# Four key chunks of an attention projection computed as seven block products in the queries' list

## The chip, the cores and the metric

The kernel runs on one core of one Trainium2 chip. A core has a matrix engine (PE, TensorE), a vector engine (DVE, VectorE), an activation engine (ACT, ScalarE), a general one (POOL, GpSimd), a queue engine that starts transfers (SP) and 16 DMA engines. Matmuls write to PSUM, eight banks of 128 partitions by 512 floats; everything else works from SBUF. The metric is the device time of one execution in microseconds, the median of several runs; less is better.

## The reference

One inference step of a decoder trunk with two layers, in float32, on 512 prompt tokens and 8 x 4 new tokens of sequences that have 256 tokens behind them. All 544 tokens go through the weights together.

```python
# layer 0: Conformer convolution; layer 1: stick-breaking attention; each followed by a gated ConvFFN
h = rms_norm(x, norm_mix[i])
x = x + mixer(h)
h = rms_norm(x, norm_ffn[i])
x = x + (silu(causal_dwconv(h @ w_gate)) * (h @ w_up)) @ w_down

# the attention's projection: D = 1024, 16 heads of 64
qkv = (h @ attn_w_qkv[a]).reshape(b, t, 3, N_HEADS, HEAD_DIM)
z = einsum('bqhd,bkhd->bhqk', q, k) * HEAD_DIM ** -0.5 + bias      # strictly causal
log_fail = where(valid, log_sigmoid(-z), 0)
after = cumsum(log_fail, axis=3, reverse=True) - log_fail
out = einsum('bhqk,bkhd->bqhd', exp(log_sigmoid(z) + after), v)
```

The rows of K and V of all new tokens are outputs. The 8 sequences attend to their past through a paged cache: 16 pages of K and 16 of V, each 128 tokens by 1024 numbers.

## The kernel before

**Operands.** Tokens stand in the free dimension: `xT`, `XH` and `XL` are 128 partitions x 8 chunks x 544 tokens. A float32 product is made from three matmuls of a faster type: weights are split into `whi` (a rounded copy by ScalarE, line 397) and `wlo` (the rest, by VectorE, line 400), the input into `XH` and `XL`, and `whi XH + whi XL + wlo XH` is summed in PSUM. A chunk of 128 outputs with 1024 inputs takes 8 x 3 matmuls for each of two token stretches, `SA` (256 columns) and `SB` (288).

**Weights.** `raws` is the list of loads, 1 MB each for a pair of chunks, through two SBUF buffers (`RAW_BUFS`); a load is started on SP (line 360) as soon as the last split of the load two places ahead has read its buffer. `specs` is the list of splits, through five buffers (`SPLIT_BUFS`). `both` enters two plain splits for a pair, `quad` four for a pair in the seven-product form.

**Seven products.** `products` (in `ffn`) computes a pair of chunks from a 2 x 2 division: input chunks 0 to 3 and 4 to 7, the two output chunks of the pair, and tokens 0 to 271 and 272 to 543. Sums of weight blocks (`sums`, VectorE) and of token blocks (`inputs`, giving `TH` and `TL`) go through seven products of 12 matmuls with 272 columns; three PSUM tiles hold them, and `put` combines them: a ScalarE copy, or a VectorE addition onto what is there. A plain pair takes 96 matmuls, this one 84. The ConvFFN's chunks and query chunks 4 to 7 (`query_quad`) are made so; query chunks 0 to 3 are plain (`PLAINQ`).

**Order.** The work of a stage is collected as operations in a `Plan`, which orders them before the program is written by estimated costs, readiness and the length of the chain behind each; the order of each engine is then fixed. The first ConvFFN and `queries` (its last product, the norm, the queries) are one list. A second list, the attention list, follows with a plan of its own that starts as if all engines were free. It holds: the projections of keys and values as matmuls that fill gaps (`project`, `plan.fill`, lines 2125 to 2127; order in `TURNS`); `keys` (copy to `kT`, then `to_rows`: turned by PE into the one PSUM bank `one`, copied by VectorE to one of two tiles `kr`, line 2169, and stored); `page_logits` (each of 16 K pages gathered by POOL into one of three tiles, line 2017, turned in two halves into the one bank `t`, line 2245, copied by VectorE or ScalarE, line 2252, and multiplied, line 2263); `decode_weights`; the prompt's attention by pairs of heads (`pair`: logits `z`, line 2387, exponentials, scans on VectorE, line 2417, weights turned in `t`, line 2429, products with V, line 2449); and `sequence`, the V pages. The second ConvFFN follows.

The splits that the attention list needs first are prepared by the end of the queries' list, since each finished weight slot prepares the one five places on (`used`).

Of the kernel before, what the change touches and what calls it, by code (L numbers as in the profile page):

```python
# [19 lines left out]
NC = D // P  # L20
SEQ = 512
# [21 lines left out]
MORE = 3  # L43
CONV_RAWS = 12
PLAINQ = 4

PASSES = ((0, 4), (4, 6), (10, 6), (16, 6))
FFN_CHUNKS = 6
# [4 lines left out]
U_POST = 1.0  # L53
# [196 lines left out]
def tile_trunk(  # L250
# [9 lines left out]
    dve, act, pool, pe = nc.vector, nc.scalar, nc.gpsimd, nc.tensor  # L260
# [35 lines left out]
    def quad(w, c):  # L296

        raws.append(cols2(w, 0, NC, c))
        specs.extend((len(raws) - 1, k, k == 4, NC) for k in (0, 2, 3, 4))
# [29 lines left out]
    for c in range(0, NC, 2):  # L329
        if c < PLAINQ:  # L330
            both(attn_w_qkv[0], 0, NC, c)
        else:
            quad(attn_w_qkv[0], c)
    TURNS = [("k", 0), ("k", 1), ("v", 0)] + [x for c in range(NC) for x in (("k", c + 2), ("v", c + 1)) if x[1] < NC]
    kv = {}
    for f, c in TURNS:
        if (f, c // 2) not in kv:
# [380 lines left out]
    plan = Plan(E_CONV, 0.12, CONV_SHIFTS)  # L718
# [384 lines left out]
    for c in range(0, NC, 2):  # L1103
        pt = psum("av")
# [196 lines left out]
    def ffn(l, before, after):  # L1301
# [455 lines left out]
        def queries(s):  # L1757
# [115 lines left out]
            for c2 in range(PLAINQ, NC, 2):  # L1873
                query_quad(c2, range(s, s + 4))
                s += 4
            xs = [("x", c, h) for c in range(NC) for h in range(2)]
            plan.op("sp", 5.0, lambda: nc.sync.dma_start(out=xsave, in_=xflat), r=[*xs, "normed1"], w=["saved"])
            plan.op("dve", 0.6, decode_columns, w=["tables"])
# [221 lines left out]
    def dcost(n):  # L2100
        return 0.09 + n * 1.1e-3

    def acost(n):
        return 0.1 + n * 0.95e-3
# [54 lines left out]

    def keys(c, h):  # L2160
        c0, n = (SA, SB)[h]
        pt = project(k0 + TURNS.index(("k", c)), h)
        plan.op("act", acost(256), lambda: act.copy(kT[:, c, c0:c0 + 256], pt()[:, :256]),  # L2163
                r=[pt], w=[("k", c, h)] + ([("ktp", i) for i in range(4)] if c >= 4 else []))
        if h:
            plan.op("act", 0.2, lambda: act.copy(kT_s[:, c, :], pt()[:, 256:n]), r=[pt], w=[("kT_s", c)])
        rows, src = to_rows(lambda b: kT[:, c, c0 + b * P:c0 + (b + 1) * P], [("k", c, h)])
        kr = sbuf("kr", 2 * P, 2)
        plan.op("dve", 0.38, lambda: dve.tensor_copy(kr().rearrange("p (b d) -> p b d", b=2), src()), r=[rows], w=[kr])
        plan.op("sp", 3.0, lambda: nc.sync.dma_start(out=kpv[:, 2 * h:2 * h + 2, c * P:(c + 1) * P],  # L2170
                                                     in_=kr().rearrange("p (b d) -> p b d", b=2)), r=[kr])
# [408 lines left out]
```

## Time and profile before

Three runs took 1270.61 to 1270.97 us, median 1270.66. The profile is of one execution; it gives its span, from the first to the last instruction, and no time beside it.

| | us |
|---|---|
| median of the runs | 1270.66 |
| span of the profiled execution | 1268.1 |
| PE, DVE, ACT busy in it | 1257.2, 1004.7, 717.5 |
| 600.0 to 633.5: last part of the queries' list | 33.5 |
| 633.5 to 723: attention list until the decode weights are turned | 89.5 |
| 723 to 845: rest of the attention list | 122 |

A row of the profile names engine, line of the kernel, operation, output and inputs. A matmul's duration (0.28 us) is longer than the step to the next (0.12 us), since matmuls are pipelined: a PE that shows as busy may still be waiting a little between two of them. What counts is the distance between starts. A wait is put down to the engine that released it.

### The profile page before, as it was taken

To read this page: it belongs to the slowest core of one execution; us is meant where nothing else is said; L and a number is where in the kernel's file an instruction comes from. 1 tells how busy PE (TensorE), PEld (TensorE's weight loads), DVE (VectorE), ACT (ScalarE), POOL (GpSimd) and SP (SyncE) were. 2 spreads that over 40 slices of the span, in tenths; PEclk is the share of its full clock that TensorE was granted. 3 is DMA by queue.
4 is the path that set the end of the run, shared out by engine and by line. 5 is a ranking of instruction groups with operands and counts; after the bars stand their busy time and mean duration, and the time that the engine had idled before them with its cause. 6 is when DMAs were issued, how large, how long until landed. Compare 5 with 4: busy or idle time off the path is not lost.

```text
span 1268.1 us, 26470 instructions
## 1 busy us (share of the span) xinstructions
PE 1257.2 (99%) x10846; PEld 1207.7 (95%) x10846; DVE 1004.7 (79%) x1696; ACT 717.5 (57%) x1436; POOL 166.0 (13%) x291
## 2 busy tenths in 40 slices
PE   9999999999999999999999999999999999999998
PEld 8997699999999999999989888999999999999998
DVE  7999876979987887869865589766988987886863
ACT  7794584635655455445564598754646645455453
POOL 5000014101001000002042143200111001000000
PEclk9999999999999999999999999999999999999999
DMA  7455423133233233244354443342123233232221
GB/s 221 131 165 156 119 69 115 35 100 102 92 112 99 74 112 115 62 144 172 116 185 154 152 144 132 119 145 73 62 85 117 91 96 117 67 119 91 85 77 72
DMA packets 119179, 142.39 MB, mean 112 GB/s; under 512 B 5101, under 2 KB 110245, under 8 KB 118786
## 3 DMA queue, kind: packets, MB, share of 16 engines
q1 hardware_dynamic: 110350, 111.89, 28.2%
q0 software_dynamic: 8704, 28.80, 7.0%
q8 instruction: 85, 1.39, 0.5%
q14 instruction: 36, 0.29, 0.1%
q10 hardware_dynamic: 4, 0.01, 0.0%
HBM read 129.34 MB, written 12.18 MB: 112 GB/s over the span
## 4 chain that ended last, share of the span: by engine, by line
PE 88%; DVE 9%; ACT 1%; issue 1%; DMA 0%; DVEq 0%; ACTq 0%
PE acc L1627 5%; PE acc L1626 5%; PE acc L1625 5%; PE acc L755 4%; PE acc L756 4%; PE acc L757 4%; PE av L892 3%; PE tr L1627 3%; PE tr L1626 3%; PE tr L1625 3%; PE av L1401 3%; PE av L1402 3%; PE av L1403 3%; PE tr L1401 3%; PE tr L1402 3%; PE tr L1403 3%
## 5 line engine op out<-in xcount | busy, mean ns | idle before, releaser
L397 ACT CAST whi<-raw 128x1024 fp32r<-128x1024 f32 (+2 forms) x247 | 224.3, 912 | 122.2 <-PE av L1402 25.1
L400 DVE TENSOR_TENSOR wlo<-raw,whi 128x1024 fp32r<-128x1024 f32 (+2 forms) x247 | 259.1, 1052 | 26.6 <-ACT whi L397 24.9
L755 PE MATMUL acc<-XH,whi 128*128 128x288 f32 (+1 forms) x384 | 112.7, 294 | 0.0
L757 PE MATMUL acc<-XH,wlo 128*128 128x288 f32 (+1 forms) x384 | 110.3, 287 | 0.9 <-DVE wlo L400 0.9
L756 PE MATMUL acc<-XL,whi 128*128 128x288 f32 (+1 forms) x384 | 110.3, 287 | 0.0
L1401 PE MATMUL av<-HH,whi 128*128 128x288 f32 (+1 forms) x280 | 83.3, 298 | 0.4 <-DVE xT L1716 0.4
L1627 PE MATMUL acc<-TH,wlo 128*128 128x272 f32 x288 | 83.0, 288 | 0.0
L1626 PE MATMUL acc<-TL,whi 128*128 128x272 f32 x288 | 82.7, 287 | 0.0
L1625 PE MATMUL acc<-TH,whi 128*128 128x272 f32 x288 | 82.7, 287 | 0.0
L1402 PE MATMUL av<-HL,whi 128*128 128x288 f32 (+1 forms) x280 | 82.6, 295 | 0.0
L2125 PE MATMUL acc<-XH,whi 128*128 128x256 f32 (+1 forms) x264 | 82.0, 311 | 0.6 <-ACT kT L2163 0.6
L1403 PE MATMUL av<-HH,wlo 128*128 128x288 f32 (+1 forms) x280 | 82.3, 294 | 0.0
L1661 ACT COPY G<-acc 128x272 f32<-128x272 f32 (+1 forms) x72 | 26.8, 372 | 94.7 <-PE acc L1627 94.7
L1401 PE MATMUL tr<-HH,whi 128*128 128x256 f32 (+1 forms) x280 | 79.1, 283 | 0.0
L1402 PE MATMUL tr<-HL,whi 128*128 128x256 f32 (+1 forms) x280 | 78.9, 282 | 0.0
L1403 PE MATMUL tr<-HH,wlo 128*128 128x256 f32 (+1 forms) x280 | 78.5, 280 | 0.0
L2127 PE MATMUL acc<-XH,wlo 128*128 128x256 f32 (+1 forms) x264 | 75.8, 287 | 0.0
L2126 PE MATMUL acc<-XL,whi 128*128 128x256 f32 (+1 forms) x264 | 75.8, 287 | 0.0
L755 PEld LDWEIGHTS acc<-XH,whi 128*128 128x128 f32 x384 | 72.2, 188 | 1.4 <-issue 0.4
L757 PEld LDWEIGHTS acc<-XH,wlo 128*128 128x128 f32 x384 | 72.1, 188 | 1.1 <-DVE wlo L400 1.1
L756 PEld LDWEIGHTS acc<-XL,whi 128*128 128x128 f32 x384 | 72.2, 188 | 0.3
L1564 DVE SCALAR_TENSOR_TENSOR cv<-G,fprm,cv 128x560 f32<-128x560 f32 x88 | 69.5, 797 | 0.5
(465 smaller groups left out, 4372.7 us busy)
## 6 DMA issues: line engine op xcount, KB each, us to landing
raw<-in_ffn_w_gate_dram SPq DMA_DIRECT2D x22, 1024.0 KB
raw<-in_ffn_w_up_dram SPq DMA_DIRECT2D x22, 1024.0 KB
raw<-in_ffn_w_down_dram SPq DMA_DIRECT2D x24, 768.0 KB
raw<-in_attn_w_qkv_dram SPq DMA_DIRECT2D x12, 1024.0 KB
raw<-in_conv_w_in_dram POOLq DMA_DIRECT2D x6, 1024.0 KB, 8.7
rep<-glu SPq DMA_DIRECT2D x36, 142.0 KB
raw<-in_conv_w_out_dram POOLq DMA_DIRECT2D x4, 1024.0 KB, 7.0
raw<-in_ffn_w_down_dram SPq DMA_DIRECT2D x8, 512.0 KB
```

What stands on the lines that cost most here:

```text
L397: act.copy(hi[:, k, :], src[:, k])
L400: dve.tensor_tensor(lo[:, k, :], src[:, k], hi[:, k, :], op=ALU.subtract)
L755: pe.matmul(o, hi[:, k, :], XH[:, k, c0:c0 + n], start=(k == 0), stop=False)
L756: pe.matmul(o, hi[:, k, :], XL[:, k, c0:c0 + n], start=False, stop=False)
L757: pe.matmul(o, lo[:, k, :], XH[:, k, c0:c0 + n], start=False, stop=(k == NC - 1))
L1401: pe.matmul(o, hi[:, j + k, :], xh, start=(start and k == 0), stop=False, **kw)
L1402: pe.matmul(o, hi[:, j + k, :], xl, start=False, stop=False, **kw)
L1403: pe.matmul(o, lo[:, j + k, :], xh, start=False, stop=(stop and k == len(xs) - 1), **kw)
L1625: pe.matmul(o, hi[:, j + k, :], xh, start=(start and k == 0), stop=False, **kw)
L1626: pe.matmul(o, hi[:, j + k, :], xl, start=False, stop=False, **kw)
L1627: pe.matmul(o, lo[:, j + k, :], xh, start=False, stop=(k == 3), **kw)
L2125: pe.matmul(o, hi[:, k, :], XH[:, k, c0:c0 + n], start=(k == 0), stop=False)
```

## The change

Key chunks 0 to 3 leave the attention list's projections and are made at the end of the queries' list as two pairs of seven block products, right behind the query pairs. They use the token-half sums `TH` and `TL` that the query pairs use. `key_quad` copies and combines the products into `kT`, and copies the new tokens' columns to `kT_s`. The turning of the key rows for the output and their store stay in the attention list; for these chunks they now have nothing to wait for there.

```diff
+EARLY_K = 4
...
+    for c in range(0, EARLY_K, 2):
+        quad(attn_w_qkv[0], NC + c)
-    TURNS = [("k", 0), ("k", 1), ("v", 0)] + [x for c in range(NC) for x in (("k", c + 2), ("v", c + 1)) if x[1] < NC]
+    TURNS = [("v", 0)] + [x for c in range(NC) for x in (("k", c + 2), ("v", c + 1))
+                          if x[1] < NC and (x[0] == "v" or x[1] >= EARLY_K)]
...
+            def key_quad(c2, slots):
+                def put(what, p):
+                    what = what.split()
+                    i, h = (int(x) - 1 for x in what[-1])
+                    c, (c0, n) = c2 + i, HALVES[h]
+                    dst = lambda: att["kT"][:, c, c0:c0 + n]
+                    w = [("kT", c, h)]
+                    if what[0] == "keep" or what[0] == "12":
+                        plan.op("act", acost(n), lambda: act.copy(dst(), p()[:, :n]), r=[p], w=w, urgent=U_POST)
+                    else:
+                        plan.op("dve", dcost(n), lambda: dve.tensor_tensor(
+                            dst(), p()[:, :n], dst(), op=SIGN[what[0]]), r=[p], w=w, urgent=U_POST)
+
+                products(slots, (("acc",) * 3, ("tr", "av", "tr"))[c2 // 2 % 2], put)
+                for c in (c2, c2 + 1):
+                    plan.op("act", 0.2, lambda c=c: act.copy(att["kT_s"][:, c, :], att["kT"][:, c, SEQ:]), r=[("kT", c, 1)])
+
+            for c2 in range(0, EARLY_K, 2):
+                key_quad(c2, range(s, s + 4))
+                s += 4
...
     def keys(c, h):
         c0, n = (SA, SB)[h]
-        pt = project(k0 + TURNS.index(("k", c)), h)
-        plan.op("act", acost(256), lambda: act.copy(kT[:, c, c0:c0 + 256], pt()[:, :256]),
-                r=[pt], w=[("k", c, h)] + ([("ktp", i) for i in range(4)] if c >= 4 else []))
-        if h:
-            plan.op("act", 0.2, lambda: act.copy(kT_s[:, c, :], pt()[:, 256:n]), r=[pt], w=[("kT_s", c)])
+        if c >= EARLY_K:
+            pt = project(k0 + TURNS.index(("k", c)), h)
+            plan.op("act", acost(256), lambda: act.copy(kT[:, c, c0:c0 + 256], pt()[:, :256]),
+                    r=[pt], w=[("k", c, h)] + ([("ktp", i) for i in range(4)] if c >= 4 else []))
+            if h:
+                plan.op("act", 0.2, lambda: act.copy(kT_s[:, c, :], pt()[:, 256:n]), r=[pt], w=[("kT_s", c)])
```

Up to the first query products the order of every engine is as before, and from the end of the attention list on too. Three places in between. In the rows, lines of the new kernel from `keys` on are 25 or 26 higher; numbers behind names tell buffers apart.

PE, from the end of the queries' list to the first pages (`acc`: a projection; `one`: rows of K turned; `z`: logits; `t`, `dz`: halves of a page). Before:

```order
L1627 MATMUL av_7965<-THq,wlo_7923 128x272
L2125 MATMUL acc_8072<-XH,whi_7941 128x256
...
L2127 MATMUL acc_8097<-XH,wlo_7942 128x288
L2245 MATMUL t_8105<-ident,xT 128x128 x4
L2245 MATMUL dz_8110<-ident,xT 128x128 x4
L2155 MATMUL one_8116<-ident,kT 128x128 x2
L2125 MATMUL acc_8097<-XH,whi_7941 128x288
...
L2127 MATMUL acc_8097<-XH,wlo_7942 128x288
L2245 MATMUL t_8130<-ident,xT 128x128 x4
```

And now:

```order
L1631 MATMUL tr_8197<-THq,wlo_8140 128x272
L2180 MATMUL one_8306<-ident,kT 128x128 x2
L2413 MATMUL z_8309<-kT,qT 128x512
L2413 MATMUL z_8311<-kT,qT 128x512
L2180 MATMUL one_8316<-ident,kT 128x128 x2
L2271 MATMUL t_8322<-ident,xT 128x128 x4
L2271 MATMUL dz_8327<-ident,xT 128x128 x4
L2180 MATMUL one_8333<-ident,kT 128x128 x2
L2271 MATMUL t_8340<-ident,xT 128x128 x4
L2180 MATMUL one_8346<-ident,kT 128x128 x2
L2271 MATMUL t_8352<-ident,xT 128x128 x4
L2150 MATMUL acc_8358<-XH,whi_8159 128x256
```

Thirty projection matmuls stood ahead of the first page half, and six behind the first row turn; now the first projection comes after ten rows of turns and logits.

VectorE, at the same place (`wlo`: a weight split; `kr`: the copy of turned key rows). Before:

```order
L400 TENSOR_TENSOR wlo_7993<-raw_7926,whi_7992 128x1024
L1867 SCALAR_TENSOR_TENSOR qT<-av_7965,qT 128x272
L400 TENSOR_TENSOR wlo_8023<-raw_7963,whi_8022 128x1024
L400 TENSOR_TENSOR wlo_8027<-raw_7926,whi_8026 128x1024
L2252 COPY kT<-t_8105 128x4x128
L2169 COPY kr_8127<-one_8116 128x256
```

And now:

```order
L404 TENSOR_TENSOR wlo_8192<-raw_8042,whi_8191 128x1024
L1891 TENSOR_TENSOR kT<-tr_8197,kT 128x272
L404 TENSOR_TENSOR wlo_8225<-raw_8144,whi_8224 128x1024
L1891 TENSOR_TENSOR kT<-tr_8197,kT 128x272
L404 TENSOR_TENSOR wlo_8257<-raw_8195,whi_8256 128x1024
L404 TENSOR_TENSOR wlo_8261<-raw_8144,whi_8260 128x1024
L2195 COPY kr_8313<-one_8306 128x256
L2195 COPY kr_8319<-one_8316 128x256
L2278 COPY kT<-t_8322 128x4x128
L2195 COPY kr_8338<-one_8333 128x256
L2278 COPY kT<-t_8340 128x4x128
```

In both orders the last splits of the queries' list stand ahead of the first copies of the attention list; the copies are now two of key rows ahead of the first page half.

PE, at the end of the stretch with the K pages (`t` from `e`: a block of the prompt's weights turned; the `dz` row: the page logits). Before:

```order
L2245 MATMUL t_8964<-ident,xT 128x128 x4
L2125 MATMUL acc_8940<-XH,whi_8500 128x256
...
L2127 MATMUL acc_8940<-XH,wlo_8501 128x256
L2429 MATMUL t_8983<-ident,e_8439 128x128 x4
L2125 MATMUL acc_8988<-XH,whi_8500 128x288
...
L2127 MATMUL acc_8988<-XH,wlo_8501 128x288
L2429 MATMUL t_9002<-ident,e_8439 128x128 x4
L2263 MATMUL dz_8802<-kT,xT 32x256 x8
```

And now:

```order
L2271 MATMUL t_8984<-ident,xT 128x128 x4
L2150 MATMUL acc_8959<-XH,whi_8256 128x288
...
L2152 MATMUL acc_8959<-XH,wlo_8257 128x288
L2271 MATMUL t_8998<-ident,xT 128x128 x4
L2271 MATMUL t_9010<-ident,xT 128x128 x4
L2455 MATMUL t_9017<-ident,e_8560 128x128 x4
L2289 MATMUL dz_8878<-kT,xT 32x256 x8
```

Twelve projection matmuls stood between the turns; now the last two halves and a block of weights follow each other.

## The prediction

> **What bounds the kernel now.** I read the head of the page first, then the chain, then the stages around the change.
>
> ```profile
> span 1268.1 us, 26470 instructions
> PE 1257.2 (99%) x10846; PEld 1207.7 (95%) x10846; DVE 1004.7 (79%) x1696; ACT 717.5 (57%) x1436; POOL 166.0 (13%) x291
> PE 88%; DVE 9%; ACT 1%; issue 1%; DMA 0%; DVEq 0%; ACTq 0%
> 620.00:633.50 13.50, 13.01 (x104) 12.79 (x103) 9.28 (x12) 7.80 (x13) 0.66 (x3) 1.00 0.47 157
> 633.50:640.00 6.50, 6.50 (x57) 6.50 (x56) 4.22 (x6) 3.56 (x5) 4.54 (x6) 1.00 0.33 109
> 640.00:680.00 40.00, 40.00 (x349) 34.41 (x348) 27.75 (x38) 26.82 (x46) 12.38 (x15) 1.00 0.51 164
> 680.00:723.00 43.00, 42.45 (x396) 38.76 (x394) 18.26 (x29) 17.36 (x35) 8.81 (x10) 1.00 0.55 169
> 723.00:845.00 122.00, 121.48 (x1314) 107.64 (x1313) 98.81 (x148) 95.64 (x172) 34.02 (x39) 1.00 0.43 140
> PE acc L2125 <- ACT kT L2163: 0.6, 1, 0.6
> ```
>
> The stage rows give, after the colon, length, PE, PEld, DVE, ACT and POOL busy, clock, DMA share, GB/s. PE is the bound: 88% of the chain, and full in every stage. The queries' list ends at 633.5; the attention list follows. From 633.5 to 723, where the 16 key pages are turned, the list of waits has a single one on PE, 0.6 us (last row). So each matmul less is worth its issue time, but only while PE keeps something to issue: VectorE and ScalarE are under 70% busy there because projection matmuls lie between the dependent steps. That filling is what the change takes away.
>
> **What a matmul costs.** PE rows of the timeline, start and duration:
>
> ```profile
> 625.23 0.28 PE L1625 MATMUL av<-THq,whi 128*128 128x272 f32 x1
> ...
> 629.60 0.29 PE L1627 MATMUL av<-THq,wlo 128*128 128x272 f32 x1
> ...
> 630.38 0.40 PE L1625 MATMUL av<-XH,whi 128*128 128x272 f32 x1 [0.49 <-ACT qT L1865]
> ...
> 633.50 0.28 PE L2125 MATMUL acc<-XH,whi 128*128 128x256 f32 x1
> ...
> 637.13 0.60 PE L2245 MATMUL t<-ident,xT 128*128 128x128 f32 x4
> 637.56 0.60 PE L2245 MATMUL dz<-ident,xT 128*128 128x128 f32 x4
> 638.00 0.38 PE L2155 MATMUL one<-ident,kT 128*128 128x128 f32 x2
> ...
> 644.79 1.13 PE L2387 MATMUL z<-kT,qT 64*128 64x512 f32 x4
> 645.85 0.66 PE L2245 MATMUL t<-ident,xT 128*128 128x128 f32 x4
> ```
>
> From 625.23 to 629.60 lie 35 steps: 0.125 us for 272 columns, the mean of the 256 and 288 that a chunk's two stretches have. A chunk pair took 2 x 48 = 96 matmuls, 12.0 us, and takes 7 x 12 = 84, 10.5 us. Two pairs save 24 matmuls: **-3.0 us**. The order of PE's program has exactly 24 rows fewer, so the change does what it says. What the products add elsewhere is priced by these rows (min/median/max, ns):
>
> ```profile
> L1364 DVE TENSOR_TENSOR Sq<-raw x2: 1217/1218/1218, 601.8 to 617.5; 128x1024 f32<-128x1024 f32 x2
> L1367 DVE TENSOR_TENSOR raw<-Sq,raw x2: 684/685/686, 606.8 to 619.3; 128x512 f32<-128x512 f32 x2
> L400 DVE TENSOR_TENSOR wlo<-raw,whi 128x1024 fp32r<-128x1024 f32 x6 | 7.3, 1222 | 0.5 <-ACT whi L397 0.5
> L397 ACT CAST whi<-raw 128x1024 fp32r<-128x1024 f32 x7 | 7.4, 1051 | 3.3 <-DVE raw L1369 1.2 <-PE av L1402 0.8 <-ACT whi L397 0.5
> L1867 DVE SCALAR_TENSOR_TENSOR qT<-acc,qT x3: 432/434/434, 615.4 to 624.4; 128x272 f32<-128x272 f32 x3
> L1865 ACT ACTIVATE qT<-acc x4: 384/395/401, 610.8 to 622.4; 128x272 f32<-128x272 f32 x4
> ```
>
> A pair asks VectorE for sums 1.22 + 2 x 0.69, splits 3 x 1.22 + 0.69 and three combinations of 0.43: 8.2 us, and ScalarE for casts 3 x 1.05 + 0.6, four copies of 0.39 and two small ones: 5.7. Both fit into the 10.5 us of PE: hidden, and if the cover failed, only the excess would cost. The 0.49 us wait at 630.38 (an accumulator read by ScalarE before its next addition) moves from the last query pair to the last key pair: nothing.
>
> **The start of the attention list.** It was 30 projection matmuls (3.6 us from 633.50) and then the pages. Now it starts with the ten rows of PE's order shown with the change, and no projection stands between them. `one` and `t` have one PSUM bank each, so the second `one` waits for VectorE's copy of the first. In VectorE's order (shown there too) that copy stands behind the splits wlo_8257 and wlo_8261, and the raw load of the former starts only when wlo_8192 has given its buffer back. Before, the same lag was there, and PE had projections to run:
>
> ```profile
> 626.44 1.23 DVE L400 TENSOR_TENSOR wlo<-raw,whi 128x1024 fp32r<-128x1024 f32 x1
> 634.06 2.44 DVE L400 TENSOR_TENSOR wlo<-raw,whi 128x1024 fp32r<-128x1024 f32 x2
> 638.42 0.42 DVE L2169 COPY kr<-one 128x256 f32<-128x256 f32 x1
> 632.82 2.00 ACT L397 CAST whi<-raw 128x1024 fp32r<-128x1024 f32 x2 [0.21 <-DMA raw<-in_attn_w_qkv_dram]
> 820.81 1.62 DMA out_dram<-vtok
> ```
>
> The split that ended at 626.44 + 1.23 = 627.67 freed a raw buffer, and the cast of the next load waited until 632.82: 5.15 us for a load. With T the end of the last product (633.5 + 168 x 0.125 = 654.5): wlo_8192 writes the buffer of the split five slots back, last read 60 matmuls before T (T - 7.5). Cast 1.05, split 1.22, about 0.2 of queue: done at T - 5.0; load landed T + 0.2; cast T + 1.2; splits T + 2.5 and T + 3.7; first copy T + 4.15. PE reaches the second `one` at T + 0.22 + 1.06 = T + 1.3 and waits until T + 4.2: **+2.9**. Bounds: 1.6 if only the last split is late (its buffer is read until T), 5 if the load takes 2 us more.
>
> For a single-bank tile, what is the shortest time from start to start?
>
> ```profile
> 659.96 0.66 PE L2245 MATMUL t<-ident,xT 128*128 128x128 f32 x4
> 661.47 0.60 PE L2245 MATMUL t<-ident,xT 128*128 128x128 f32 x4
> 662.75 0.66 PE L2245 MATMUL t<-ident,xT 128*128 128x128 f32 x4
> 660.65 0.69 DVE L2252 COPY e<-t 128x512 f32<-128x512 f32 x1 [0.93 <-PE t L2245]
> 662.11 0.59 ACT L2252 COPY e<-t 128x512 f32<-128x512 f32 x1
> ...
> 824.50 0.49 ACT e L2432
> ```
>
> The middle page half starts at 661.47, ScalarE copies it from 662.11 for 0.59, and the next starts at 662.75: 0.64 + 0.59 + 0.05 = 1.28, the closest pair that the trace of before has. By VectorE (0.69) it is 1.38, and 1.18 for a turned block of weights (0.49, last row). With these, VectorE's 0.42 for a row copy and 1.6 for a store (the 1.62 above; the third row copy needs the first one's store landed), the chain runs: second `one` T + 4.2, its copy to 5.0, the first half's copy to 5.7; third row copy to 6.6; second half from 5.75, copied 6.65 to 7.35 behind it; last half 7.4; first projection T + 7.9. The rows' own work is 3.7: 4.2 lost, so **+1.3** beyond the first wait (0.7 to 2).
>
> **The pages.** Until the weights of decode are turned, before had 46 us of projections between 32 page halves, now 26. The third piece of the order shows the end of that stretch: two halves and a block back to back, where twelve projections stood between each two. A block of four takes 0.44 (637.13 to 637.56), so back to back they ask for 0.44 between starts, and six matmuls of 256 columns between them make 1.15. Down the whole order behind the start: eight pairs at 1.15 (short by 0.13 or 0.23), four at 1.23 (0.05 or 0.15), two with only a row turn between (0.50 each), two back to back (0.94 and 0.84): 1.4 + 0.4 + 1.0 + 1.8 = **+4.6**; before, one pair is short by 0.05. Bounds: 2.8 (the last four alone) and 6.6 (0.15 more for each). Page gathers are not the limit:
>
> ```profile
> DMA to landing us min/median/max: 4.2/5.5/8.4
> ```
>
> From a page's last use to its buffer's next, PE has 5.8 us of work or more, save for page 3 (4.3, and the waits above make it 5.8): nothing, up to 0.8.
>
> Sum: -3.0 + 2.9 + 1.3 + 4.6 = **+5.8 us**: the profiled span would go from 1268.1 to 1273.9. The median shown, 1270.66, lies 2.6 above the span; the same 2.6 gives **1276.5**. After the pages both orders have 600 rows of PE with the same steps, so nothing returns what was lost.
>
> **The clock.** It was granted in full in the stages above; it fell only at the very end:
>
> ```profile
> 1260.00:1268.00 8.00, 2.31 (x20) 1.98 (x18) 2.09 (x5) 1.36 (x3) 0.98 (x1) 0.77 0.34 131
> ```
>
> PE idle for 5.7 of 8 us came with 0.77. [...]
>
> **The rivals.** (1) *Hidden stalls only*: the load lands early, VectorE has no backlog, and the pairs with projections between them cost nothing; left are the four close pairs, 2.8, and 0.7 at the start: +0.5, 1271.2. For it: VectorE is 42 to 69% busy there. Against: the splits wait for PE's own last products. (2) *The full gain* on the other side: PE finds each copy done, as at every page pair of before; -3.0, 1267.7. It is faster as long as all waits together stay below 0.5 us; from 3.0 on nothing is left. Against it stand the two pairs back to back, which alone cost 1.8. (3) *VectorE's order*: page copies now also queue behind scans.
>
> ```profile
> 650.05 2.34 DVE L2417 TENSOR_TENSOR_SCAN s<-ones,s 128x512 f32<-128x512 f32 x2 [0.93 <-ACT s L2408]
> ```
>
> Three page copies follow scans directly in its new order; with half such a pair waited at each, 1.2 us, +3.5: 1280.0. (4) *The clock gates*, for PE idle about 3 us at T: the end row's missing 0.23 over one more 8 us would be 1.8, 1278.3.
>
> **How the numbers follow.** A change under 0.2%, 2.5 us, cannot be told from none here. The sum as it stands or nearly has 0.55, its own range 1273.5 to 1279 (bounds of the start and the pairs, not all at once); the clock rival 0.07, VectorE's order 0.10: slower 0.72 in all. Hidden stalls: 0.21, within 0.2%. Full gain: 0.07, faster. The range 1271 to 1280.5 leaves out the full gain, the lowest part of rival 1 and what of rival 3 and of the bounds lies above.
>
> **What would show it.** Right: at about 654 a wait of PE on VectorE's `kr` copy of 2 to 4 us; PE waits on VectorE's and ScalarE's page copies where before has none; PE busy below 95% from 655 to 720; the stretch behind it as long as before. Wrong in the sum: PE full at 655 (no backlog), or page halves closer than 1.28 us (a shorter turnaround). If the product stretch itself is longer than 21 us, VectorE did not hide the sums. If the time is 1267.7, the copies were never late, and the reading of the order was wrong altogether.

## The result and the profile after

The changed kernel takes **1285.63 us** (median of 4 runs, 1285.30 to 1286.91), the kernel before 1270.63 (4 runs, 1269.91 to 1270.97): a ratio of 1.0123, 95% interval 1.0111 to 1.0135. It is slower by 15.0 us, where 5.8 were predicted. The sign was right, the size was not, and 1285.6 lies outside the range.

The profiled executions differ by more, 17.1 us. Every execution takes 1.7 us more than its span. The profile of the change is of its longest one (1286.91), that of before (1268.1 + 1.7 = 1269.8) of a short one; 1.3 and 0.8 us of the 17.1 are this choice. The head of the page of the change:

```profile
span 1285.2 us, 26447 instructions
PE 1262.4 (98%) x10822; PEld 1208.1 (94%) x10822; DVE 1014.1 (79%) x1712; ACT 720.3 (56%) x1440; POOL 165.6 (13%) x291
```

24 matmuls fewer, as said, and yet 5.2 us more of TensorE's busy time. The stages of the change, to be laid beside those of before in the prediction (after the colon: length; PE, PEld, DVE, ACT, POOL busy; granted clock, DMA share, GB/s):

```profile
620.00:633.50 13.50, 13.50 (x110) 13.50 (x109) 12.34 (x16) 7.60 (x13) 0.28 (x1) 1.00 0.25 79
655.00:660.00 5.00, 2.33 (x16) 1.50 (x12) 3.81 (x5) 2.94 (x4) 0.00 (x0) 0.94 0.14 25
660.00:665.00 5.00, 1.50 (x8) 1.00 (x6) 0.86 (x2) 0.44 (x1) 0.98 (x1) 0.50 0.97 340
665.00:670.00 5.00, 5.00 (x27) 4.79 (x25) 1.28 (x3) 0.58 (x1) 0.95 (x1) 0.54 0.49 154
670.00:727.00 57.00, 55.08 (x490) 45.52 (x488) 32.81 (x48) 30.47 (x52) 18.41 (x21) 1.00 0.52 153
727.00:734.00 7.00, 4.16 (x47) 2.59 (x48) 3.91 (x7) 4.46 (x10) 1.60 (x3) 1.00 0.88 296
734.00:738.50 4.50, 4.50 (x21) 3.34 (x20) 3.58 (x7) 2.97 (x5) 0.51 (x1) 0.62 0.04 13
738.50:860.00 121.50, 120.66 (x1310) 107.05 (x1309) 96.53 (x146) 93.83 (x171) 34.04 (x39) 1.00 0.42 132
```

Up to 654 nothing is lost. Then there are two holes, 655 to 665 and 727 to 734. In the first the granted clock falls to 0.50 at about 659.4, behind the second at about 734.4. At 665 to 670 PE counts as busy all the time, but its steps are about twice as long (0.215 us from 666.34 on, 0.12 from 670.25 on). The rows of the first hole, of all engines by start (start and duration):

```profile
654.12 0.29 PE L1631 MATMUL tr<-THq,wlo 128*128 128x272 f32 x1
654.24 0.38 PE L2180 MATMUL one<-ident,kT 128*128 128x128 f32 x2
654.52 1.99 ACT L401 CAST whi<-raw 128x1024 fp32r<-128x1024 f32 x2 [0.94 <-DMA raw<-in_attn_w_qkv_dram]
655.60 2.36 DVE L404 TENSOR_TENSOR wlo<-raw,whi 128x1024 fp32r<-128x1024 f32 x2 [0.72 <-ACT whi L401]
657.88 0.42 DVE L2195 COPY kr<-one 128x256 f32<-128x256 f32 x1
657.99 0.37 SPq L364 DMA_DIRECT2D raw<-in_attn_w_qkv_dram  x1
658.35 0.44 PE L2180 MATMUL one<-ident,kT 128*128 128x128 f32 x2 [2.67 <-DVE kr L2195]
658.41 7.76 SPq L2196 DMA_DIRECT2D out_dram<-kr  x4
664.14 0.42 DVE L2195 COPY kr<-one 128x256 f32<-128x256 f32 x1 [4.19 <-DMA out_dram<-kr]
664.62 0.69 PE L2180 MATMUL one<-ident,kT 128*128 128x128 f32 x2 [3.50 <-DVE kr L2195]
665.98 0.56 PE L2150 MATMUL acc<-XH,whi 128*128 128x256 f32 x1
666.34 0.42 PE L2151 MATMUL acc<-XL,whi 128*128 128x256 f32 x1
```

The products end on time, at 654.24 (predicted 654.5). The second row turn starts at 658.35, 4.1 us later (predicted 4.2), behind exactly the two splits and the load that the prediction named. (A copy reads its PSUM bank directly: `kr<-one`. Until it is done, here at 658.30, the bank is not free for the next turn.) The second wait is new: the first row store, issued at 658.41, has landed only at 664.1. The next 1 MB of weights had been asked for on SP at 657.99, directly ahead of it, and the DMA engines are full (0.97). With two buffers for the rows, the third row copy waits for that store, the fourth row turn for the copy, and the first projection starts 11.7 us after the products instead of 7.9.

The end of the page stretch, PE's rows and ScalarE's one:

```profile
725.93 0.66 PE L2271 MATMUL t<-ident,xT 128*128 128x128 f32 x4
727.37 0.66 PE L2271 MATMUL t<-ident,xT 128*128 128x128 f32 x4 [0.78 <-DVE e L2278]
728.75 0.66 PE L2455 MATMUL t<-ident,e 128*128 128x128 f32 x4 [0.73 <-ACT e L2278]
733.19 0.64 ACT L2189 COPY kT<-acc 128x256 f32<-128x256 f32 x2
733.61 0.39 PE L2150 MATMUL acc<-XH,whi 128*128 128x256 f32 x1 [1.75 <-ACT kT L2189]
```

The two pairs back to back take 1.44 and 1.38 from start to start, 1.00 and 0.94 more than their own 0.44 (predicted 0.94 and 0.84). Then something else: a projection waits for its bank until ScalarE has copied key chunk 4 out of it. That copy writes over turned pages, so it cannot go before their product (729.3 to 730.4), and on ScalarE it stands behind three activations: two of the page logits, the first of which waits for VectorE until 731.4, and one of the prompt's logits.

The last loss is where the attention list hands over to the next one; the change first, the same row of before below it:

```profile
861.33 0.74 DVE L2559 TENSOR_TENSOR xT<-z,xT 128x256 f32<-128x256 f32 x2
862.22 0.37 PE L498 MATMUL acc<-XH,whi 128*128 128x288 f32 x1 [1.27 <-ACT sq L569]
```

```profile
845.23 0.30 PE L494 MATMUL acc<-XH,whi 128*128 128x288 f32 x1
```

**The account**, in the profiled executions. From the first row of the attention list to the first matmul of the next list before needs 211.73 us (633.50 to 845.23), of which 24.0 are the 192 projection matmuls that left it, and the change 207.98 (654.24 to 862.22): 207.98 - 187.73 = **20.25 us lost in the list**, against 8.8 predicted (4.2 + 4.6) and 3.0 saved. By place: start 8.0 (11.74 to the first projection, 3.7 of it own work); the clock behind the start about 1.8 (steps of 0.215 us instead of 0.12 until 669.7, and a turned half); page halves 5.2 (1.94 measured for the last two pairs; the other 3.3 is only what the stretch from 666 to 737 leaves beside the terms named here, and was not added up row by row); the wait for key chunk 4 2.0; the clock behind it 1.6; the next list's bank 1.5 (1.27 and the gap around it). Together 20.1, which agrees with 20.25 because the 3.3 is a remainder.

### The profile page after: what moved, and what is told of

It is laid out like the page before. It is cut to its first block, busy times and chain, and to the rows that moved or that the text cites. A ratio compares the mean times of both kernels' runs of the same rounds, so it can differ in the third digit from the quotient of the medians.

```text
span 1285.2 us, 26447 instructions
## 1 busy us (share of the span) xinstructions
PE 1262.4 (98%) x10822; PEld 1208.1 (94%) x10822; DVE 1014.1 (79%) x1712; ACT 720.3 (56%) x1440; POOL 165.6 (13%) x291
## 5 line engine op out<-in xcount | busy, mean ns | idle before, releaser
L1631 PE MATMUL acc<-XH,wlo 128*128 128x272 f32 x240 | 69.4, 289 | 0.0
L1630 PE MATMUL acc<-XL,whi 128*128 128x272 f32 x240 | 69.2, 288 | 0.0
L1629 PE MATMUL acc<-XH,whi 128*128 128x272 f32 x240 | 69.0, 287 | 0.0
```

Of the source, the lines that this page charges most:

```text
L1629: pe.matmul(o, hi[:, j + k, :], xh, start=(start and k == 0), stop=False, **kw)
L1630: pe.matmul(o, hi[:, j + k, :], xl, start=False, stop=False, **kw)
L1631: pe.matmul(o, lo[:, j + k, :], xh, start=False, stop=(k == 3), **kw)
```

## The experiments

Theory A after the result: the start's two waits, the clock that falls behind waits, the close page halves, the wait for key chunk 4 and the bank are separate causes, and each gives its time back when it is repaired. Rival C: the attention list is short of filling, so that a repaired wait lets the next dependent step wait instead. The table has, for each kernel, the difference of medians to the kernel before, the interval of the ratio on record (an estimate that can lie 0.001 beside the quotient of the medians), and the loss in the list as reckoned above (with 12.0 instead of 24.0 where one pair of key chunks is moved).

| kernel | over before, us | ratio | lost in the list |
|---|---|---|---|
| the change | +15.0 | 1.0111 to 1.0135 | 20.25 |
| plain | +17.3 | 1.0119 to 1.0152 | 18.8 |
| warm | +14.7 | 1.0096 to 1.0130 | 17.8 |
| kr4 | +13.0 | 1.0087 to 1.0121 | 14.3 |
| psfix | +14.9 (one run) | | 18.7 |
| defer | +13.0 | 1.0082 to 1.0115 | 15.5 |
| vfirst | +9.9 | 1.0062 to 1.0095 | 12.6 |
| t2 | +11.2 | 1.0077 to 1.0110 | 12.7 |
| shared0 | +11.6 | 1.0073 to 1.0107 | 15.4 |
| c2 | +8.0 | 1.0047 to 1.0080 | 11.2 |
| best | +7.9 | 1.0052 to 1.0085 | 10.6 |
| best2 | +12.3 | 1.0072 to 1.0107 | 15.8 |
| best3 | +10.4 | 1.0064 to 1.0098 | 13.8 |
| best4 | +2.9 | 1.0015 to 1.0034 | 6.1 |
| b5 | +1.5 | 1.0003 to 1.0021 | 4.9 |
| k2 (one pair) | +11.1 | 1.0070 to 1.0103 | 13.2 |
| k2b (one pair) | +4.3 | 1.0022 to 1.0047 | 6.5 |
| k2c (one pair) | +6.2 | 1.0029 to 1.0063 | 7.1 |
| b7 (one pair) | +0.1 | 0.9994 to 1.0012 | 2.2 |

### The move or the products? (plain)

```diff
     for c in range(0, EARLY_K, 2):
-        quad(attn_w_qkv[0], NC + c)
+        both(attn_w_qkv[0], 0, NC, NC + c)
...
-            for c2 in range(0, EARLY_K, 2):
-                key_quad(c2, range(s, s + 4))
-                s += 4
+            for c in range(EARLY_K):
+                for h, st in enumerate((SA, SB)):
+                    pt = group(s + c, st, NC, XH, XL, xkeys, ("acc", None)[c % 2])
...
```

(`group` is the plain projection of the first query chunks, 48 matmuls a chunk; ScalarE copies its result to kT.)

> The move without the saving: key chunks 0 to 3 are projected at the end of the queries' list as in the change, but each with 48 matmuls (four plain projections, no sums of blocks or of token halves), so PE has as many matmuls as before. The attention list is that of the change. Theory A (the loss comes from the attention list that is left without filling): the change's time and up to 3.0 us on top, 1286 to 1289. Rival D (the seven block products, with their sums and splits on VectorE, cause the late splits at the start and so most of the loss): VectorE has no backlog, the wait of 2.7 us and the clock drop behind it go, 1278 to 1282.

+17.3 against +15.0, inside theory A's range: the seven block products save about 2.3 us of the 3.0 and are not the cause. VectorE's backlog is smaller without them, but the hole is the same:

```profile
PE one L2186 <- DVE kr L2201: 5.0, 2, 3.7
PE acc L2156 <- ACT kT L2195: 1.7, 1, 1.7
PE acc L498 <- ACT sq L569: 1.3, 1, 1.3
```

(Waits of PE: total, times, longest.) The two row waits are 5.0 together instead of 6.2, the other two are the change's to the digit. The move alone, with no matmul saved, costs 17 us.

### The store wait alone (kr4)

```diff
-        kr = sbuf("kr", 2 * P, 2)
+        kr = sbuf("kr", 2 * P, 4)
```

> The changed kernel with four buffers instead of two for the key rows, so that the third row copy need not wait until the first store has landed. In the profile of the change the first projection of the attention list starts 11.7 us after the last product, of which 3.5 us are a wait of TensorE's fourth row turn on that copy. Theory A (the start of the list costs most of the miss: two waits, and behind them a clock of 0.50): the 3.5 us go, the clock stays low for a shorter time, 4 to 5 us less than the change, 1281. Rival C (the loss is the missing filling of the page stretch, wherever it shows): what the start gains is lost again at the pages, under 1.5 us less, 1284 to 1286.

PE's order is the same row for row, so this is a clean cut. The wait of 3.50 is gone, and the stages show more than that:

```profile
655.00:660.00 5.00, 2.49 (x16) 1.47 (x16) 3.90 (x6) 3.10 (x4) 0.00 (x0) 1.00 0.12 26
660.00:665.00 5.00, 4.23 (x32) 3.57 (x32) 2.22 (x5) 1.04 (x2) 1.92 (x2) 1.00 1.04 338
722.70:730.00 7.30, 4.51 (x50) 2.94 (x51) 4.22 (x8) 4.72 (x10) 1.96 (x3) 1.00 0.85 287
730.00:734.50 4.50, 4.50 (x33) 3.61 (x33) 3.58 (x6) 3.01 (x5) 0.16 (x1) 1.00 0.03 8
```

The first wait is still there, nearly as long (2.51 us), and the clock does not fall behind it. At the end of the page stretch the same waits of 0.8, 0.7 and 1.7 us stand as in the change (727 to 734 there, 722.7 to 730 here), and the clock stays at 1.00 where it was 0.62. The profile has 6 us less loss, the median only 2: two of the four executions, at a mean clock of 0.998, took 1281.2 and 1282.0, the two at 0.995 took 1283.4 and 1283.7. The executions of one program differ by about 2 us along with the clock. The median, 1282.7, lies between theory A's 1281 and rival C's 1284 to 1286.

### The clock alone (warm)

```diff
+BUSY = {(0, 0): 20, (1, 0): 24}
...
         rows, src = to_rows(lambda b: kT[:, c, c0 + b * P:c0 + (b + 1) * P], [("k", c, h)])
+        if (c, h) in BUSY:
+            busy(BUSY[c, h], rows)
```

(`busy` issues so many matmuls of 256 columns into the idle bank av, behind the row turn.)

> The changed kernel with 44 matmuls of 256 columns added whose result nobody reads: 20 behind the first row turn and 24 behind the third, where TensorE waits 2.7 and 3.5 us in the profile of the change (20 x 0.12 = 2.4 us and 24 x 0.12 = 2.9 us, so they fit into the waits). The rows of all other work keep their order. Theory A (the low clock follows from TensorE's idle time): the granted clock stays 1.00 from 655 to 725, where it was 0.50 for 10 us; the waits stay, the transposes and projections behind the second wait no longer take twice as long, about 3 us less than the change, 1282 to 1283; the second drop near 735 stays. Rival B (the low clock has another cause, such as the load of the whole chip or the DMA traffic there): the clock falls as before, and the time is 1285.6 or up to 1 us more.

```profile
660.00:665.00 5.00, 3.64 (x32) 3.40 (x30) 0.95 (x3) 0.59 (x1) 0.98 (x1) 1.00 1.00 335
665.00:670.00 5.00, 4.76 (x37) 3.98 (x36) 1.40 (x3) 1.71 (x4) 1.83 (x2) 1.00 0.49 164
```

With PE kept busy the clock stays at 1.00 at the very DMA load (1.00 and 0.49 busy, 0.97 and 0.49 in the change) at which it was 0.50: rival B, the traffic, is out. That the work kept it there fits, but one profile does not show it, for in kr4 the clock kept 1.00 without it. The second drop stays, as expected (0.77 at 730 to 735). The loss in the list falls by 2.4 us in the profile, where 3 were expected, but the difference of medians only by 0.3 and the ratio by 0.001 (1.3 us), which the two intervals do not separate. The mean clock of the change's other three executions was 0.996 to 0.997 against 0.993 in the profiled one, so there was less to win in them. The clock is a part of the loss in the profiled execution, and a small one of the median.

### The root of the start's waits (defer)

```diff
-            if s >= len(specs):
+            if s >= len(specs) or kv0 + 3 <= s < kv0 + 5:
                 return
...
+    plan.op("late raw", 3.0, lambda: None, w=[("raw", specs[k0 + 3][0])])
+    prepare(k0 + 3)
+    prepare(k0 + 4)
```

(The first line is in `used`, so the queries' list leaves these two slots out; kv0 is the first slot of `TURNS`. The others stand at the head of the attention list.)

> The changed kernel with the last two splits of weights of the queries' list (of slots that are needed 27 us later or more) moved into the attention list, where the scheduler places them. VectorE then meets the first two row copies before any split that waits for a raw load, and the next raw load is queued on SP behind the row stores, not ahead of them. Theory A (those two splits and the load behind them are the root of the start's loss): the waits of 2.7 and 3.5 us shrink to under 1 us together, the clock stays at 1.00 there; the page stretch loses as in the change: 8 to 10 us less than the change, 1275.5 to 1278. Rival C (filling is filling): the pages come earlier and lose more, 1283 to 1286. Rival F (the DMA traffic at the start is the cause, whatever stands ahead on the queues): the fourth row turn still waits for the first store, 1281 to 1284.

The named root was the right one, and the gain did not follow. PE's second and fourth row turns (the list starts at 655.80 here):

```profile
657.17 0.44 PE L2185 MATMUL one<-ident,kT 128*128 128x128 f32 x2
...
659.33 0.38 PE L2185 MATMUL one<-ident,kT 128*128 128x128 f32 x2
```

Neither waits; the whole chain of ten rows is through in 4 us, so splits and load together were the cause of both. The first store, issued at 656.80, no longer holds up the third row copy at 658.76, so rival F's wait did not come. The edit moves the load away from the store's queue and off the DMA engines at once; which of the two had kept the store, it does not tell. The median is only 2 us better than the change's. The list loses 4.8 us less, but in this profile the products end at 655.80, 1.6 later than in the change; why is not shown. The page stretch, entered earlier, loses more, and 720 to 740 holds two stages with the clock at 0.83:

```profile
720.00:730.00 10.00, 6.10 (x49) 3.22 (x48) 3.64 (x6) 4.58 (x9) 1.89 (x2) 0.83 0.66 228
```

The time is rival C's, not A's.

### The value chunk first (vfirst), one pair only (k2)

```diff
+    both_halves(values, 0)
     both_halves(keys, 0)
     both_halves(keys, 1)
-    both_halves(values, 0)
```

```diff
-EARLY_K = 4
+EARLY_K = 2
```

> The changed kernel with one edit: the first value chunk's projection stands ahead of the row turns of key chunks 0 and 1 in the one-bank ring, so 48 projection matmuls (6 us) can run while VectorE catches up and the raw loads land. Theory A: both waits at the start and the low clock behind them go, 9 us; the page stretch then has 6 us less filling and loses 2 to 4 us more than the change does: 1278 to 1281. Rival C (filling is filling): the pages lose what the start gains, 1284 to 1287.

> The change for one pair of key chunks only (0 and 1): 12 matmuls less than before instead of 24, 1.5 us. Key chunks 2 and 3 are projected in the attention list as before, so 96 projection matmuls (12 us) more than in the change lie between the pages, and six of them stand between the second and the third row turn. Theory A: the first wait on VectorE's backlog stays in part (1 to 2.7 us), the store wait is mostly covered, no clock drop, pages almost as before: 1271 to 1274. Rival C (half the filling gone, half the loss): 1270.6 plus half of 15.0, 1278.

The first repairs the start with work instead of with a cut, and is the best single edit on the two pairs: +9.9, as A said. Its 48 projections stand where the waits were, and the clock keeps 1.00 throughout the list. The second was a miss for both theories. With half the move it still loses 11.1 us, about 8 of its 13.2 in the list at the start, so the loss does not go by the amount that was moved out:

```profile
653.87 0.69 PE L2180 MATMUL one<-ident,kT 128*128 128x128 f32 x2 [4.60 <-DVE kr L2195]
```

I had taken the store wait for covered by six projections between the second and third row turn; the store is later here. It was issued at 646.05, behind two loads of 1 MB, the third row copy starts at 653.39, 7.3 us on, and the fourth turn waits even longer.

### The banks (psfix, t2, shared0)

```diff
+    for tag in ("acc", "t", "dz", "one", "z", "av"):
+        for _ in range(banks[tag]):
+            ps.tile([P, 512], F32, tag=tag, name=uid(tag), bufs=banks[tag])
```

```diff
-    banks.update(acc=2, one=1, dz=1, av=1, z=2, t=1)
+    banks.update(acc=1, one=1, dz=1, av=1, z=2, t=2)
```

> The changed kernel with the PSUM banks of the attention list laid out in the order in which the kernel before first uses them (acc, t, dz, one, z, av); no instruction is added, removed or moved. In the profile of the change the first matmul of the next list, at 862.2 us, waits 1.27 us for a bank that before got free. Theory E (the new order of first use gives the next list's accumulator a bank that is read last): that wait goes and the profiled span is 1.3 us shorter, 1283.9 beside 1285.2. Rival (the wait comes from the order of work and not from the bank): 1.27 us of wait as before, span 1285.

> The changed kernel with two PSUM banks for turned pages (t) and one for projections (acc), instead of one and two. The scheduler then makes another order: projections also stand between the first row turns. Theory A (page halves too close in one bank cost about 5 us, the start 8 and its clock 2): the page waits on VectorE's and ScalarE's copies go, and six projections cover part of the start, 6 to 9 us less than the change; each projection now waits for the copy out of its one bank wherever no other work stands between (0 to 4 us back): 1276 to 1281. Rival C (filling is filling, a bank more does not help): 1284 to 1287.

> The changed kernel with a bank that serves turned pages together with t until the page stretch ends, and the projections (acc) together with their other bank after it, so that neither is short where it is needed. The scheduler makes its own order with it; six projections then stand between the second and the third row turn. Theory A: page waits on the copies out of t go (5 us with the last two pairs), the acc wait of 1.75 us at the end of the stretch and its clock drop (2 us) go in part; the start's first wait stays, the second is half covered: 8 to 11 us less than the change, 1275 to 1278. Rival C: 1283 to 1286.

psfix changes nothing but which bank a name gets, and the handover waits no more; the span is 1283.7, close to theory E's 1283.9 (psfix's row; one run, whose time cannot show 1.3 us):

```profile
860.89 0.29 PE L498 MATMUL acc<-XH,whi 128*128 128x288 f32 x1
```

So the bank was the cause: banks are given out in the order of first use; before, a projection was first, in the change a row turn, and the next list's accumulator fell on a bank that the closing sums read last (xT<-z at 861.33). With two banks t2 shows no wait on a page copy from 670 on. Its time, 1281.75, is just above theory A's range. What is left or new are the first row wait, waits of projections and of turned value rows on ScalarE's copy out of the projections' one bank, and one page gather:

```profile
PE one L2180 <- DVE kr L2195: 2.9, 1, 2.9
PE one L2180 <- ACT vT L2203: 2.4, 3, 1.0
PE acc L2150 <- ACT vT L2203: 1.7, 2, 1.0
PE t L2271 <- DMA xT<-in_cache_k_dram,idx: 1.5, 1, 1.5
```

shared0 lends one bank to t until the pages end and to acc after that (the ring behind `psum` takes its tiles from a short list that changes once; the diff is the `phys` table and eight lines in `psum`). It gave 3.4 us of 8 to 11, and its 1281.7 lies between the two theories: the start's row waits stayed (5.1 us in all), and a turned block of pair weights waited 2.3 us at the end instead.

### Several at once (c2, best, best2)

> Four edits on the change together: four buffers for the key rows; the first value chunk projected ahead of the row turns; the fourth value chunk's projection ahead of the fifth key chunk's (so that 6 us more filling stand before the end of the page stretch, where TensorE waits 1.75 us for ScalarE's copy of the fifth key chunk, which must not overwrite the turned pages); and the PSUM banks of the attention list laid out in the order in which the kernel before first uses them. Theory A by its terms: value chunk first alone gave 1279.7 (1269.8 for before on that chip, so +9.9); the layout takes 1.3 off, the wait of 1.75 goes, the page halves at the end gain 1 to 2: +5 to +6.5, 1275 to 1276.5 where before is 1270. Rival C: +9 to +10, 1280.

> The changed kernel with four edits: the two splits moved, the shared bank, four buffers for the key rows, and the first value chunk ahead of the row turns. Theory A (the loss is the start 8 to 10, its clock, the page halves 5, the acc wait and clock at the end 4, the next list's bank 1.3, and nothing else): most of it goes, and what the 24 matmuls save shows: 1267.5 to 1271.5 where before is 1270. Rival C (the page stretch is short of filling, which no order or bank can mend): 1275 to 1280.

> As the run with all four edits, but without the first value chunk's projection put ahead: the two splits moved, the shared bank, four buffers for the key rows. Theory A: with the splits moved the row turns have nothing to wait for, so the order of the value chunk no longer matters: within 1.5 us of the run with all four, 1268 to 1273. If the first value chunk is needed as cover, 2 to 5 us more than that run.

The three came out 2.0, 6.5 and 9.3 us above the upper end of A's ranges; c2 lies between the theories, best in C's range, and best2 is the case in which the value chunk is needed. In c2 (kr4, vfirst and psfix together, with the fourth value chunk ahead of the fifth key chunk) the waits at the end of the page stretch are gone, and PE is short of work where the list ends (at 853.5), in single waits of 0.2 to 0.7 us:

```profile
838.00:858.00 20.00, 17.21 (x147) 15.09 (x146) 6.80 (x18) 5.83 (x16) 0.20 (x1) 1.00 0.38 132
```

That the 6 us of filling taken from behind are what is missing here is not shown: best4 and b5 below take the same 6 us away, and their last 15.5 us have PE full.

`best` has neither row waits nor page-copy waits of note, and yet +7.9:

```profile
PE accx L2289 <- DMA xT<-in_cache_k_dram,idx: 4.2, 3, 2.5
PE accx L2473 <- DVE e L2466: 2.0, 1, 2.0
```

The pages themselves are late now (accx is the lent bank), 4.5 to 7.8 us from issue to landing between 654 and 730. That PE asks for them faster than three page tiles can be gathered again is the likely reason; no run has a fourth tile. The first value chunk put ahead is worth 4.4 us of the medians (`best2` against `best`) though the row turns no longer wait. That would speak for C, since it is filling; but the two intervals overlap, and a part of it is the clock, which best2's profile has at 0.60 and 0.69 from 665 to 680 where best's has 1.00.

### What is left: loads, filling, or the scheduler's price (best3, best4, k2b, k2c, b5, b7)

```diff
-    plan.op("late raw", 3.0, lambda: None, w=[("raw", specs[k0 + 3][0])])
+    plan.op("late raw", 20.0, lambda: None, w=[("raw", specs[k0 + 3][0])])
...
         if c == 2:
+            both_halves(values, 3)
             decode_weights()
...
-            plan.op(f"page{i}", 4.0, lambda: None, r=[("asked", i)], w=[(t, 1)])
+            plan.op(f"page{i}", 5.5, lambda: None, r=[("asked", i)], w=[(t, 1)])
```

The first edit is in best3, best4, b5 and b7, the second (with the same swap in `TURNS`) in c2, best4, b5 and b7, the third, the time that the scheduler takes a gather for, in b5 and b7.

> As the run with four edits and two pairs, but the two moved splits are planned for 20 us after the start instead of 3, so that the raw load behind them does not run beside the page gathers of the first 15 us, where the profile shows TensorE waiting 0.8 and 2.5 us for gathered pages with the DMA share at 1.02. If the loads delay the gathers: both waits go, 2 to 3.5 us less, 1274.5 to 1276. If the gathers are late for want of a free page buffer: no change, 1278.

> As the run before it in this call, and with the fourth value chunk's projection ahead of the fifth key chunk's, so that 6 us more filling stand before the wait of 2 us at 721 us. Theory A: that wait goes, 1 to 3 us less than the run before it (1272 to 1275). Rival C: the filling is missing at the end of the list instead, no gain.

> One pair of key chunks (0 and 1) moved instead of two, with the start repaired: the last two splits moved into the attention list, four buffers for the key rows, and the PSUM banks laid out as in the kernel before. The run with one pair and nothing else lost 11 us, of which its profile shows some 9 at the start (a wait of 4.6 us on a row store and a low clock behind it) and 1.3 at the next list's bank. Theory A (the start and the bank are the loss; 12 us more filling cover the page halves): 1.5 us saved and 1 to 2 of small waits, 1269 to 1273. Rival C (any filling moved out is lost in waits): 1276 to 1280.

> As the run with four edits (two splits moved, shared bank, four row buffers, first value chunk ahead), for one pair of key chunks instead of two. Theory A: 1268.5 to 1272. Rival C: 1274 to 1277, half way between before and the same edits with two pairs (1278).

> As the run with five edits (two splits moved and planned late, shared bank, four row buffers, first value chunk ahead, fourth value chunk ahead of the fifth key chunk), and the scheduler takes a page gather for 5.5 us where it took 4.0; the trace shows 4.2 to 6.6. Projections then stand between the first pages instead of waits. Theory A: the 3.6 us of waits on gathers go in part, 1.5 to 3 us less, 1270 to 1271.5, same as before within 0.2%. Rival C (the filling put there is missing elsewhere): 1273 or more.

> As the run before it in this call, for one pair of key chunks instead of two: 12 matmuls saved (1.5 us), 12 us more filling between the pages. Theory A: waits of no more than 2 us in all are left, 1269 to 1271. Rival C: half the loss of the two pairs with the same edits, and no gain: 1271 to 1273.

best3 ruled out the loads: without them beside the gathers (the load at 661.87 in best is at 685.98 in best3) the waits on pages grew, from 4.2 to 4.8 us, and the time from +7.9 to +10.4. best4, with 6 us of filling ahead of the place where PE waited, gained 7.5 on best3, the largest step of all, in A's range and against C's "no gain". It is more than the 1 to 3 us of the wait that was aimed at: PE is busy for 20.0 us of 680 to 700 instead of 17.1 and for all of 720 to 730 instead of 6.8, and the clock, 0.78 and 0.88 from 725 to 735 in best3, stays at 1.00. What it left were gathers. With 5.5 us as a gather's price (b5; best4's gathers took 4.2 to 6.6) the scheduler put projections there: +1.5, just above A's range. One pair less moved (b7) gave 12 us more filling: +0.1, in A's range. k2b, with the start and the bank repaired and one pair, lies between the theories (+4.3); k2c is in C's range (+6.2). The longest waits of PE, b5 first:

```profile
PE accx L2289 <- DVE kT L2296: 0.7, 2, 0.5
PE one L2198 <- DVE vtok L2225: 0.6, 1, 0.6
```

```profile
PE accx L2289 <- DMA xT<-in_cache_k_dram,idx: 1.0, 1, 1.0
PE acc L1630 <- ACT kT L1890: 0.7, 1, 0.7
```

No kernel of these beats the one before. b7 equals it: 1.5 us saved, 2.2 lost in the list in waits of 1.0 us and less.

## Why the prediction was wrong in size

By its own steps, in the profiled executions:

- **-3.0 for 24 matmuls, and sums and splits hidden**: right. The products ended 0.3 us earlier than predicted, the one wait of 0.5 moved to the key pair, and plain priced the saving at about 2.3, from medians whose runs spread by 0.8 and 1.6.
- **+2.9 for VectorE's backlog**: right, 2.67, by the named splits and load; defer takes them away, and the wait with them.
- **+1.3 for the rest of the start chain**: this is the step that failed first, 3.8 us short (8.0 at the start instead of 4.2). Its one assumption was a store that lands in 1.6 us, from a row of a store with nothing ahead of it. The prediction had the last split end at T + 3.7, and by the kernel's own rule that split starts the next 1 MB load on SP, just ahead of the store; it did not ask what the store would meet. Its upper bound for the term was 2.
- **+4.6 for page halves**: nearly right as far as it is known. The last two pairs lost 1.94 where 1.8 were predicted (1.38 and 1.44 from start to start instead of 1.28 and 1.38), but the 5.2 in all has 3.3 in it that are a remainder. The sign that was named came: from 655 to 720 PE is busy for 57.3 of 65 us, 88%.
- **"Nothing returns what was lost" behind the pages**: true, but more was lost there, 2.0 for key chunk 4 and 1.5 for the bank. The first had its row in the prediction (the single PE wait of before, 0.6 us on this copy); it was read as a small thing of before, not as a wait that filling kept small. The second cannot be read from PE's order, which does not name banks.
- **The clock**, a rival with a chance of 0.07 and 1.8 us: it came, twice, 3.4 us in the profiled execution. With waits of 4.2 us forecast at one place, and a clock of 0.77 beside an idle PE at the end of before, it deserved more.
- **The base**: 2.6 us were added to the span for the median; every execution shows 1.7.

The sum, 5.8 + 3.8 + 0.6 + 3.5 + 3.4 = 17.1, is the difference of the spans; the medians' 15.0 has less of the clock in it. The common error is that each wait was priced alone on the old order. The experiments after the result made the same error: defer, best and c2 were expected to give back what their waits showed, and gave a fraction.

What the runs support lies between theory A and rival C. The move as such costs 17 us (plain). The start's waits and the bank are causes of their own, each taken away by an edit (defer, psfix), as A says; the clock's part comes and goes between executions of one program (kr4). But a wait that is taken away mostly let another step wait, at the pages or at the end, as C says. C's stronger form, that no order or bank can mend a list that is short of filling, does not hold: vfirst, best4 and b5 have as many projections in the list as the change, at other places, and with the repairs the loss in the list falls from 20.25 to 4.9 us. Where the independent matmuls stand counts, beside how many there are. This is the reading that fits the runs best. It is argued and not shown, since best to b7 join several edits, and the clock takes part in every step. How much of the gap between b7 and its saving could still be had is open; that the start, the pages and the bank were the whole of it is not shown either, since no run has all waits gone.

## What to carry to other kernels

Independent matmuls inside a list of dependent steps are not only work, they hide the steps: before moving them to save 3 us, count how many microseconds of waits they cover, on every engine and queue, and not only on the one that waits first. Before taking a store's landing time from another place, look what is issued just ahead of it: here it was 5.7 and 7.3 us behind loads of 1 MB, and at most 2.0 without one. And a repaired wait is worth its length only if the step behind it was not about to wait as well.

## What was not expected of the hardware

- **The clock fell after 2.7 us without work, and stayed after 2.9.** In the change it was 0.50 from about 659.5 to 669.7, after 655.7 to 658.4 without a matmul; with waits of 2.51 in kr4 and of 2.9 in t2, at the second row turn too, it kept 1.00 (t2's mean over the profiled execution is 0.999, the change's 0.993). The waits of 0.8, 0.7 and 1.7 us within 7 us were followed by a clock of 0.62 in the change and of 1.00 in kr4. So the length of a wait alone does not tell whether the clock falls; what else decides it, no run shows.
- **A 128 KB store took 5.7 us to land** when a 1 MB load had been issued 0.4 us before it on the same queue, 7.3 us behind two such loads (k2), and at most 2.0 with none ahead of it (defer). The prediction's 1.6 is of a store of 256 KB with nothing ahead. The DMA engines were also full at the time (0.97 at 660 to 665 in the change); whether they kept the store or the load ahead of it on the queue, no run parts.
